# A scale chain issued in two halves around a down column tile, and two pieces of work of the first block pairs written later

## The chip, the cores and the metric

One core of a Trainium2 chip runs the whole program. The metric is device time of one execution in microseconds (us), the median of three runs. Engines are named as in the profile: PE is TensorE (matmul), DVE is VectorE, ACT is ScalarE, POOL is GpSimd, SP is SyncE, which issues most of the DMAs here.

## The reference, cut to what matters

The kernel computes one layer of a streaming encoder on 512 tokens of width 2048: a mixer (a gated recurrence and a band attention), and then a gated feed-forward block with a causal convolution of width 3. Only the second part is touched by the change:

```python
h2 = rms_norm(x, g_ffn[l])
up = causal_dwconv(h2 @ w_up[l], conv_w[l], conv_b[l])      # 2048 -> 2 * 5632
a, gate = jnp.split(up, 2, axis=-1)
x = x + (a * jax.nn.silu(gate)) @ w_down[l]                 # 5632 -> 2048
```

## The kernel before, in words

The feed-forward width 5632 is cut into 44 pairs of 128 channels (128 of `a` and the 128 of `gate` that belong to them). Pairs 0 to 3 are plain: `lead()` multiplies them in f32, and `lead_taps` (L1014) does their convolution taps and gating. Pairs 4 to 43 are block pairs, one `up_unit` each (L988): a product scheme that needs seven `product` calls of 24 matmuls with 256 columns in place of eight. Four pairs make a group, which gives one row block of `w_down`; a group is multiplied in eight down tiles, `down(g, c2)` (L1059), each two column tiles of 12 matmuls with 512 columns. From unit 5 on the order of the steps is fixed as unit, two down tiles, unit, two down tiles and so on (L1086 to L1095); one unit with its two down tiles is called a period here. The last ten down tiles follow unit 43.

All these matmuls run in f16 as a high and a low part. For this every weight tile is split by `split16` (L886): ACT writes the high half (L889), DVE the low half (L890). The scale of a split comes from the largest absolute row sum of the tiles that share it, found by a **scale chain**, `period_scales` (L914): six ACT passes over whole tiles with `accum_out` (`abs_sums`, L895; four tiles of the unit, two raw down tiles, which it loads itself through SP, L876), then in `scales` (L763) a DVE reduction (L770), a diagonal on ACT (L771), one PE product with a matrix of ones (L773) that spreads the sums over the partitions, and small DVE operations (L774 to L776). `m_scale` (L846) does the same for a finished group, and its splits are `m_split` (L853). A tile called `dg` holds the diagonals, in a pool of one buffer; raw down tiles have a pool of three buffers, tag `raw`.

What sets the order: the Python lists `todo`, `ready` and `later`. `todo` holds closures in the order of consumption, nine per period: `start` (the scale chain if the unit has no scale yet, and the split of tile a22), the splits of a11, s1, s2, a12, s4, s3, and the splits of the period's two down tiles. Each closure appends one split tile to `ready`. `take(n)` (L864) runs closures until `ready` has n + 1 entries, and hands out the first:

```python
def take(n_ahead):
    while len(ready) < 1 + n_ahead and todo:
        todo.pop(0)()
    return ready.pop(0)
```

Every `product` (L980) and every `down` (L1060) calls `take(3)`. `start` (L942) reads:

```python
def start():
    if "s" not in u:
        period_scales(j, ds)
    whl("a22")
```

The dict `u` of a unit gets its "s" in `period_scales` alone (L933). `later` is popped once at the end of every product (L985); the taps of pairs 2 and 3 and the scaling of finished groups go through it. The framework schedules each engine's instructions by their place in the program and by when they are ready, and it sets all waits; a tile's buffer goes to the next tile of its tag when its last user is done.

Of the kernel before, what the change touches and what calls it, by code (L numbers as in the profile page):

```python
# [52 lines left out]
def block_kernel(ctx: ExitStack, tc: tile.TileContext, xT, wst, cols, bias_t, masks, yT):  # L53
# [76 lines left out]
    def mm3(ps, sh, sl, mh, ml, start, stop):  # L130
        PE.matmul(ps, lhsT=sh, rhs=mh, start=start, stop=False)  # L131
        PE.matmul(ps, lhsT=sh, rhs=ml, start=False, stop=False)  # L132
        PE.matmul(ps, lhsT=sl, rhs=mh, start=False, stop=stop)  # L133


    colt = cst.tile([P, NC], F32, name="colt")
# [623 lines left out]

    def scales(sets, bound):  # L763


        n = len(sets)
        t = sm_t()
        dg = dgp.tile([P, 2, P], BF16, tag="dg", name=nm("dg"))
        for i, r in enumerate(sets):
            V.tensor_reduce(out=t[:, i:i + 1], in_=r, axis=mybir.AxisListType.X, op=ALU.max)  # L770
            A.activation(dg[:, i], ident, AF.Copy, scale=t[:, i:i + 1])  # L771
        psm = c3(mx_t()[:, 0:2 * P], 2)
        PE.matmul(psm[:, 0:n], lhsT=on1b, rhs=dg[:, 0:n], start=True, stop=True)  # L773
        V.tensor_reduce(out=t[:, 2:2 + n], in_=psm[:, 0:n], axis=mybir.AxisListType.X, op=ALU.max)  # L774
        V.tensor_scalar(out=t[:, 4:4 + n], in0=t[:, 2:2 + n], scalar1=1.01 / bound, scalar2=1e-30, op0=ALU.mult, op1=ALU.add)
        V.reciprocal(out=t[:, 6:6 + n], in_=t[:, 4:4 + n])  # L776
        return [(t[:, 4 + i:5 + i], t[:, 6 + i:7 + i]) for i in range(n)]
# [86 lines left out]
# [4 lines that stand above are left out]
# [25 lines left out]
    def abs_sums(r, tiles):  # L893
        for k, t in enumerate(tiles):
            A.activation(junk_t(), t, AF.Abs, accum_out=r[:, k:k + 1])  # L895
# [13 lines left out]
    def down_loads(ds):  # L909
        at_end = DOWNS.index(ds[0]) - N_BESIDE  # L910
        new = ur_t if at_end >= 0 and at_end % 4 == 0 else raw_t
        return [load(new(), N_DOWN + 8 * g + c2) for g, c2 in ds]

    def period_scales(j, ds):  # L914

        r = sm_t()
        sets = []
        u = units.get(j)
        if u is not None:
            abs_sums(r[:, 0:4], [u[n] for n in ("s1", "a22", "a11", "a12")])  # L920
            sets.append(r[:, 0:4])
        if ds:
            raws = down_loads(ds)
            abs_sums(r[:, 4:8], raws)
            sets.append(r[:, 4:4 + len(ds)])
        sc = scales(sets, BND)
        dt = [(raw, *sc[-1]) for raw in raws] if ds else []
        if u is not None:
            h = cwp.tile([P, 1], F32, tag="uh", name=nm("uh"))
            V.tensor_tensor(out=h, in0=sc[0][0], in1=inv_h, op=ALU.mult)  # L930
            cw = cwp.tile([P, 2, 3], F32, tag="cw", name=nm("cw"))
            A.activation(cw, c3(colt[:, C_CW:C_CW + 3 * 88], 2)[:, :, 3 * j:3 * j + 3], AF.Copy, scale=h)
            u.update(s=sc[0][1], cw=cw, ds=dt)  # L933
        return dt

    def plan_unit(j, ds):
        u = units.setdefault(j, {})

        def whl(n):
            ready.append(split16(u[n], u["s"]))  # L940

        def start():  # L942
            if "s" not in u:
                period_scales(j, ds)
            whl("a22")

        def s2():
            V.tensor_tensor(out=u["a11"], in0=u["s1"], in1=u["a11"], op=ALU.add)  # L948
            whl("a11")

        def s4():
            V.tensor_tensor(out=u["a12"], in0=u["a11"], in1=u["a12"], op=ALU.add)
            whl("a12")
            if j + 1 < NPAIR_FF:
                unit_loads(j + 1)

        def s3():
            i = N_MIX + 16 + 4 * (j - N_LEAD)
            u["s3"] = load_sum(raw_t() if j == N_LEAD else spare, i, i + 2)
            whl("s3")  # L960

        todo.extend([start, lambda: whl("a11"), lambda: whl("s1"), s2, lambda: whl("a12"), s4, s3])
        todo.extend([lambda k=k: down_split(u["ds"][k]) for k in range(len(ds))])

    def down_split(d):
        raw, inv, s = d
        ready.append((split16(raw, s), inv))

    def plan_downs(ds):

        st = []

        def one(k):
            if k == 0:
                st.extend(period_scales(None, ds))
            down_split(st[k])
        todo.extend([lambda k=k: one(k) for k in range(len(ds))])

# [35 lines left out]
    def lead_taps(j, u, out=None):  # L1014
        ys = [taps(u[e], ct, colt[:, C_CW + 3 * ct:C_CW + 3 * ct + 3]) for e, ct in enumerate((j, NPAIR_FF + j))]
        gated(j, *ys, u[0], out=out)
# [7 lines left out]
    def lead():  # L1024
        half = N_LEAD // 2
        n = 0
        for j in range(half):
            u = c3(ur_t(), 2)
            for e in range(2):
                ps = mm_t()  # L1030
                for h in range(2):
                    wh, wl = next_w()
                    for k in range(8):
                        cs = slice(k * P, (k + 1) * P)
                        kt = 8 * h + k
                        mm3(ps, wh[:, cs], wl[:, cs], hh[kt], hl_[kt], kt == 0, kt == KT - 1)
                        if n == 0 and k == 3:
                            finish_r2()
                    if n in (2, 4, 6):
                        t_prep(n // 2 - 1)  # L1040
                    n += 1
                evict_r2(ps, u[:, e])
            lead_taps(j, [u[:, 0], u[:, 1]], (ssa, rmask)[j])
        unit_loads(N_LEAD)
        pss = [mm_t() for _ in range(2 * half)]
        for i in range(8):
            wh, wl = next_w()
            for e, kt in enumerate((i, i + 8)):
                for c in range(2 * half):
                    cs = slice((4 * e + c) * P, (4 * e + c + 1) * P)  # L1050
                    mm3(pss[c], wh[:, cs], wl[:, cs], hh[kt], hl_[kt], i + e == 0, i + e == 8)
            if i in (1, 2, 4, 6, 7):
                t_prep((0, 3, 4, 0, 5, 0, 6, 7)[i])
            if i == 4:
                period_scales(N_LEAD, [])
        us = [evict_r2(ps, actp.tile([P, T], F32, tag="act", name=nm("u"))) for ps in pss]
        later.extend([lambda j=j: lead_taps(half + j, us[2 * j:2 * j + 2]) for j in range(half)])

    def down(g, c2):  # L1059
        t, inv_w = take(3)  # L1060
        mg, parts = groups[g]
        inv = cwp.tile([P, 1], F32, tag="inv", name=nm("inv"))
        V.tensor_tensor(out=inv, in0=inv_w, in1=mg[:, 1:2], op=ALU.mult)
        for cc in range(2):
            c = 2 * c2 + cc
            last = g == NGRP - 1
            ps = mx_t()
            cuts = [slice(0, T)] if not last or c < KT - 1 else [slice(0, H), slice(H, T)]
            pss = [ps] if len(cuts) == 1 else [ps, mx_t()]
            for ps, ts_ in zip(pss, cuts):  # L1070
                for k in range(4):
                    cs = slice((cc * 4 + k) * P, (cc * 4 + k + 1) * P)
                    cl = slice(1024 + (cc * 4 + k) * P, 1024 + (cc * 4 + k + 1) * P)
                    m = parts[k]
                    mm3(ps[:, ts_], t[:, cs], t[:, cl], m[:, ts_], m[:, T + ts_.start:T + ts_.stop], k == 0, k == 3)
            eng = nc.gpsimd if c < KT - 3 else nc.sync
            for ps, ts_ in zip(pss, cuts):
                V.scalar_tensor_tensor(out=acc[c][:, ts_], in0=ps[:, ts_], scalar=inv, in1=acc[c][:, ts_], op0=ALU.mult, op1=ALU.add)  # L1078
                if last:
                    eng.dma_start(out=yT[c][:, ts_], in_=acc[c][:, ts_])  # L1080
# [20 lines left out]
    for st in steps:  # L1101
        if isinstance(st, tuple):
            down(*st)
            continue
        up_unit(st)
        if st == N_LEAD:
            m_scale(0)
            for j in range(4):
                m_split(j)
        elif st % 4 == 3:  # L1110
            g = st // 4
            later.append(lambda g=g: (m_scale(g), m_split(4 * g)))
            later.extend([lambda j=j: m_split(j) for j in range(4 * g + 1, 4 * g + 4)])
        if st == NPAIR_FF - 1:
            while later:
                later.pop(0)()


def _level_masks(np):
# [121 lines left out]
```

## Time and profile before

| | us |
|---|---|
| median of three runs | 2281.39 (2280.96 to 2282.54) |
| the profiled execution, its own time | 2279.07 |
| its span, first to last instruction | 2277.3 |
| stretch 1689.3 to 1808.7 of it | 119.40: four periods |

The own time of the profiled execution is 1.8 us above its span, which is what lies around the program's instructions. Times in the views are counted from the start of the span. The feed-forward part begins near 900 us, the block pairs at 1010.65, and the stretch with steady periods runs from 1089 to 2190.

### The profile page before, as it was taken

To read this page: it belongs to the slowest core of one execution; us is meant where nothing else is said; L and a number is where in the kernel's file an instruction comes from. 1 tells how busy PE (TensorE), PEld (TensorE's weight loads), DVE (VectorE), ACT (ScalarE), POOL (GpSimd) and SP (SyncE) were. 2 spreads that over 40 slices of the span, in tenths; PEclk is the share of its full clock that TensorE was granted. 3 is DMA by queue.
4 is the path that set the end of the run, shared out by engine and by line. 5 is a ranking of instruction groups with operands and counts; after the bars stand their busy time and mean duration, and the time that the engine had idled before them with its cause. 6 is when DMAs were issued, how large, how long until landed. Compare 5 with 4: busy or idle time off the path is not lost.

```text
span 2277.3 us, 34675 instructions
## 1 busy us (share of the span) xinstructions
PE 2200.5 (97%) x13667; PEld 1694.6 (74%) x13667; DVE 1672.4 (73%) x2729; ACT 1336.8 (59%) x2119; POOL 271.3 (12%) x261
## 2 busy tenths in 40 slices
PE   9999999999999999998999999999999999999989
PEld 7888888788888888785667777776776777777654
DVE  7678658857658744787777777787877777778764
ACT  5455445545445424457676767776667776767661
POOL 5223123310001103100000000000000000000001
PEclk9999999999999999999999999999999999999999
DMA  6222222232222333445555565555555666655532
GB/s 211 88 70 75 84 93 65 77 99 84 86 91 93 125 117 101 129 140 131 166 158 164 161 162 162 158 157 153 148 164 158 167 167 167 158 156 160 149 91 83
DMA packets 82755, 294.21 MB, mean 129 GB/s; under 512 B 9568, under 2 KB 10208, under 8 KB 82592
## 3 DMA queue, kind: packets, MB, share of 16 engines
q1 hardware_dynamic: 68112, 240.34, 32.4%
q0 software_dynamic: 14480, 51.65, 12.0%
q8 instruction: 107, 1.75, 0.3%
q14 instruction: 56, 0.46, 0.1%
HBM read 287.76 MB, written 4.19 MB: 128 GB/s over the span
## 4 chain that ended last, share of the span: by engine, by line
PE 49%; DVE 28%; ACT 11%; issue 6%; DMA 6%; POOL 0%; SPq 0%; ACTq 0%; DVEq 0%; POOLq 0%
PE mm L131 12%; PE mm L133 12%; PE mm L132 12%; DVE whl L890 8%; DMA raw<-wst 5%; ACT junk L895 4%; ACT whl L889 4%; DVE vo L1078 3%; PE mx L133 3%; PE mx L131 3%; PE mx L132 3%; DVE vo L828 2%; DVE vo L829 2%; DVE ur L948 1%; ACT dg L771 1%
## 5 line engine op out<-in xcount | busy, mean ns | idle before, releaser
L131 PE MATMUL mm<-th,whl 128*128 128x256 f16 x2240 | 612.5, 273 | 5.9 <-ACT whl L889 5.9
L133 PE MATMUL mm<-th,whl 128*128 128x256 f16 x2240 | 612.3, 273 | 2.6 <-DVE whl L890 2.6
L132 PE MATMUL mm<-tl,whl 128*128 128x256 f16 x2240 | 612.3, 273 | 0.0
L131 PE MATMUL mm<-act,whi 128*128 128x512 f32 x1024 | 406.4, 397 | 0.0
L133 PE MATMUL mm<-act,wlo 128*128 128x512 f32 x1024 | 399.4, 390 | 0.0
L131 PEld LDWEIGHTS <-whl 128*128 128x128 f16 x2948 | 289.1, 98 | 147.9 <-issue 32.0
L132 PE MATMUL mm<-act,whi 128*128 128x512 f32 x1024 | 398.8, 389 | 0.0
L133 PEld LDWEIGHTS <-whl 128*128 128x128 f16 x2948 | 289.2, 98 | 133.7 <-issue 22.5
L132 PEld LDWEIGHTS <-whl 128*128 128x128 f16 x2948 | 289.2, 98 | 108.5 <-issue 0.8
L889 ACT ACTIVATE whl<-ur,sm 128x1024 f16<-128x1024 f32 x206 | 231.1, 1142 | 154.2 <-DVE ur L948 52.1
L119 ACT CAST whi<-raw 128x1024 fp32r<-128x1024 f32 (+1 forms) x161 | 167.7, 1042 | 228.9 <-PE mm L132 183.7
L890 DVE SCALAR_TENSOR_TENSOR whl<-ur,sm,whl 128x1024 f16<-128x1024 f32 x206 | 261.4, 1277 | 41.0 <-ACT whl L889 41.0
L122 DVE TENSOR_TENSOR wlo<-raw,whi 128x1024 fp32r<-128x1024 f32 (+1 forms) x161 | 209.5, 1302 | 91.5 <-ACT whi L119 86.7
L131 PE MATMUL mx<-mhl,whl 128*128 128x512 f16 x708 | 268.5, 379 | 0.0
L132 PE MATMUL mx<-mhl,whl 128*128 128x512 f16 x708 | 268.4, 379 | 0.0
L133 PE MATMUL mx<-mhl,whl 128*128 128x512 f16 x708 | 268.2, 379 | 0.0
L133 PEld LDWEIGHTS mm<-act,wlo 128*128 128x128 f32 x1024 | 192.2, 188 | 41.2
L131 PEld LDWEIGHTS mm<-act,whi 128*128 128x128 f32 x1024 | 192.4, 188 | 38.8 <-issue 0.5
L132 PEld LDWEIGHTS mm<-act,whi 128*128 128x128 f32 x1024 | 192.5, 188 | 38.1 <-issue 0.5
L895 ACT ACTIVATE junk<-ur 128x1024 f16<-128x1024 f32 x146 | 152.1, 1044 | 0.0
L1078 DVE SCALAR_TENSOR_TENSOR vo<-mx,inv,vo 128x512 f32<-128x512 f32 x177 | 130.3, 741 | 25.1 <-PE mx L133 25.1
L890 DVE SCALAR_TENSOR_TENSOR whl<-raw,sm,whl 128x1024 f16<-128x1024 f32 x83 | 106.3, 1283 | 43.1 <-ACT whl L889 42.2
(285 smaller groups left out, 3022.7 us busy)
## 6 DMA issues: line engine op xcount, KB each, us to landing
raw<-wst SPq DMA_DIRECT2D x242, 512.0 KB, 3.5
ur<-wst SPq DMA_DIRECT2D x146, 512.0 KB, 3.5
spare<-wst SPq DMA_DIRECT2D x59, 512.0 KB, 4.8
ur<-wst POOLq DMA_DIRECT2D x40, 512.0 KB, 5.6
spare<-wst POOLq DMA_DIRECT2D x39, 512.0 KB, 8.0
vo<-xT SPq DMA_DIRECT2D x16, 256.0 KB, 5.3
vo<-xT POOLq DMA_DIRECT2D x16, 256.0 KB, 3.1
yT<-vo POOLq DMA_DIRECT2D x13, 256.0 KB, 2.3
```

The lines of the kernel that those rows point to most:

```text
L119: A.copy(out=hi[:, c], in_=raw[:, c])
L122: V.tensor_tensor(out=lo[:, c], in0=raw[:, c], in1=hi[:, c].bitcast(F32), op=ALU.subtract)
L131: PE.matmul(ps, lhsT=sh, rhs=mh, start=start, stop=False)
L132: PE.matmul(ps, lhsT=sh, rhs=ml, start=False, stop=False)
L133: PE.matmul(ps, lhsT=sl, rhs=mh, start=False, stop=stop)
L771: A.activation(dg[:, i], ident, AF.Copy, scale=t[:, i:i + 1])
L828: V.scalar_tensor_tensor(out=y[:, 1:], in0=u[:, :T - 1], scalar=cw[:, 1:2], in1=y[:, 1:], op0=ALU.mult, op1=ALU.add)
L829: V.scalar_tensor_tensor(out=y[:, 2:], in0=u[:, :T - 2], scalar=cw[:, 0:1], in1=y[:, 2:], op0=ALU.mult, op1=ALU.add)
L889: A.activation(t[:, 0:1024], x, AF.Copy, scale=s)
L890: V.scalar_tensor_tensor(out=t[:, 1024:], in0=x, scalar=s, in1=t[:, 0:1024], op0=ALU.mult, op1=ALU.subtract)
L895: A.activation(junk_t(), t, AF.Abs, accum_out=r[:, k:k + 1])
L1078: V.scalar_tensor_tensor(out=acc[c][:, ts_], in0=ps[:, ts_], scalar=inv, in1=acc[c][:, ts_], op0=ALU.mult, op1=ALU.add)
```

## The change

The scale chain is cut into `period_sums` (load the raw down tiles, six sums) and `period_scales` (the rest). For units 6 to 43 a call of `period_sums` is added to the closure of the period's second down tile, and the result is kept in `sums_of`. A call of `period_scales` with it is added in `down`, for the first of a period's two down tiles, behind the matmuls of its first column tile; the product L773 of that call gets an ordering edge behind the last of these matmuls. `start` still computes what it finds missing. The first down tile calls `take(1)` in place of `take(3)`. The taps of pairs 2 and 3 are put further down in `later`, and the scaling of group 0 goes there too; the scaling of group 10 comes after down tiles 77 and 78 in place of directly behind unit 43.

```diff
     def mm3(ps, sh, sl, mh, ml, start, stop):
...
-        PE.matmul(ps, lhsT=sl, rhs=mh, start=False, stop=stop)
+        return PE.matmul(ps, lhsT=sl, rhs=mh, start=False, stop=stop)
...
-    def scales(sets, bound):
+    def scales(sets, bound, after=None):
...
-        PE.matmul(psm[:, 0:n], lhsT=on1b, rhs=dg[:, 0:n], start=True, stop=True)
+        with tc.issue_after(after.ins) if after is not None else ExitStack():
+            PE.matmul(psm[:, 0:n], lhsT=on1b, rhs=dg[:, 0:n], start=True, stop=True)
...
-    def period_scales(j, ds):
+    def period_sums(j, ds):
         r = sm_t()
         u = units.get(j)
         if u is not None:
             abs_sums(r[:, 0:4], [u[n] for n in ("s1", "a22", "a11", "a12")])
...
+        raws = down_loads(ds) if ds else []
+        abs_sums(r[:, 4:8], raws)
+        return j, r, raws
+
+    def period_scales(state, after=None):
+        j, r, raws = state
+        u = units.get(j)
+        sets = ([r[:, 0:4]] if u is not None else []) + ([r[:, 4:4 + len(raws)]] if raws else [])
+        sc = scales(sets, BND, after)
+        dt = [(raw, *sc[-1]) for raw in raws]
...
         def start():
             if "s" not in u:
-                period_scales(j, ds)
+                period_scales(period_sums(j, ds))
             whl("a22")
...
-        todo.extend([lambda k=k: down_split(u["ds"][k]) for k in range(len(ds))])
+        for k in range(len(ds)):
+            todo.append(lambda k=k: down_split(u["ds"][k]))
+        if ds and j + 1 < NPAIR_FF:
+            def sums(f=todo.pop()):
+                f()
+                sums_of[j + 1] = period_sums(j + 1, DOWNS[2 * (j - N_LEAD):2 * (j - N_LEAD) + 2])
+            todo.append(sums)
+
+    sums_of = {}
...
-        later.extend([lambda j=j: lead_taps(half + j, us[2 * j:2 * j + 2]) for j in range(half)])
+        later.extend([lambda: None] * 3)
+        later.append(lambda: lead_taps(half, us[0:2]))
+        later.extend([lambda: None] * 3)
+        later.append(lambda: lead_taps(half + 1, us[2:4]))
+        later.append(lambda: (m_scale(0), m_split(0), m_split(1)))
+        later.append(lambda: (m_split(2), m_split(3)))
 
     def down(g, c2):
-        t, inv_w = take(3)
+        i = DOWNS.index((g, c2))
+        first = i % 2 == 0 and i < N_BESIDE - 2
+        t, inv_w = take(1 if first else 3)
...
-                    mm3(ps[:, ts_], t[:, cs], t[:, cl], m[:, ts_], m[:, T + ts_.start:T + ts_.stop], k == 0, k == 3)
+                    last_mm = mm3(ps[:, ts_], t[:, cs], t[:, cl], m[:, ts_], m[:, T + ts_.start:T + ts_.stop], k == 0, k == 3)
+            if first and cc == 0:
+                j = N_LEAD + 2 + i // 2
+                period_scales(sums_of.pop(j), last_mm)
...
             down(*st)
+            if st in DOWNS[N_BESIDE - 1:N_BESIDE + 1] and later:
+                later.pop(0)()
+                while later and st == DOWNS[N_BESIDE]:
+                    later.pop(0)()
             continue
         up_unit(st)
-        if st == N_LEAD:
-            m_scale(0)
-            for j in range(4):
-                m_split(j)
-        elif st % 4 == 3:
+        if st % 4 == 3:
...
-        if st == NPAIR_FF - 1:
-            while later:
-                later.pop(0)()
```

`N_LEAD` is 4, `NPAIR_FF` 44 and `N_BESIDE` 78; `product` is not in the diff.

## Rows read from the trace of the kernel before

**Rows 1.** The page, section 1: the span, and each engine's busy time, share and instructions.

```profile
span 2277.3 us, 34675 instructions
...
PE 2200.5 (97%) x13667; PEld 1694.6 (74%) x13667; DVE 1672.4 (73%) x2729; ACT 1336.8 (59%) x2119; POOL 271.3 (12%) x261
```

**Rows 2.** What PE waited for (us, times, longest) in 1005:1089, then 1089:2190, then 2190:2278.

```profile
PE mm L131 <- ACT whl L889: 5.9, 3, 3.3
PE mm L133 <- DVE whl L890: 2.6, 2, 1.6
PE mx L773 <- ACT dg L771: 2.1, 3, 1.5
...
PE mx L773 <- ACT dg L771: 35.0, 30, 2.0
...
PE mx L773 <- ACT dg L771: 9.7, 1, 9.7
```

**Rows 3.** Busy us (instructions) of PE, PEld, DVE, ACT, POOL; granted clock; DMA share; GB/s.

```profile
1689.30:1808.70 119.40, 116.68 (x878) 85.67 (x877) 94.29 (x143) 83.75 (x126) 6.99 (x8) 1.00 0.58 161
...
1010.00:1089.00 79.00, 68.41 (x528) 53.06 (x527) 59.07 (x92) 56.42 (x90) 4.70 (x6) 0.94 0.59 161
...
2203.30:2213.40 10.10, 4.63 (x12) 1.73 (x12) 6.85 (x15) 5.60 (x11) 0.00 (x0) 0.50 0.12 44
```

**Rows 4.** PE in order of time in one period: first product, end of the sixth, L773.

```profile
1702.72 0.27 PE L131 MATMUL mm<-th,whl 128*128 128x256 f16 x1
...
1718.33 0.27 PE L133 MATMUL mm<-th,whl 128*128 128x256 f16 x1
1718.85 0.27 PE L773 MATMUL mx<-dg,on1b 128*128 128x256 bf16 x1 [0.25 <-ACT dg L771]
```

**Rows 5.** The chain of waits from one L773 to the next: start us, us, what.

```profile
1689.73 0.18 PE mx L773
...
1690.91 1.14 ACT whl L889
...
1693.95 1.19 DVE whl L890
...
1699.41 0.66 DVE vo L1078
...
1702.52 1.13 DVE ur L948
...
1710.37 1.29 DVE whl L890
...
1711.68 5.33 DMA raw<-wst
...
1717.03 1.15 ACT junk L895 x2
1718.18 0.63 ACT dg L771 x2
...
1718.85 0.28 PE mx L773
```

**Rows 6.** DVE in order of time, same period: split of the second raw down tile.

```profile
1713.48 1.28 DVE L890 SCALAR_TENSOR_TENSOR whl<-raw,sm,whl 128x1024 f16<-128x1024 f32 x1 [1.83 <-ACT whl L889]
```

**Rows 7.** ACT's groups in the four periods 1689.3:1808.7 (busy us, mean ns).

```profile
L895 ACT ACTIVATE junk<-ur 128x1024 f16<-128x1024 f32 x14 | 14.6, 1043 | 0.0
...
L771 ACT ACTIVATE dg<-ident,sm 128x128 bf16<-128x128 f32 x10 | 3.7, 394 | 0.0
```

**Rows 8.** Loads to landing: raw tiles in those four periods; unit tiles, whole span (median).

```profile
DMA to landing us min/median/max: 5.0/5.7/8.3
...
ur<-wst SPq DMA_DIRECT2D x146, 512.0 KB, 3.5
```

**Rows 9.** PE in order of time behind the last unit: the product of group 10's scale.

```profile
2208.77 0.27 PE L773 MATMUL mx<-dg,on1b 128*128 128x128 bf16 x1 [9.67 <-ACT dg L771]
```

More of the change, by code (lines that the diff above doesn't have):

```diff
@@ L912, in down_loads @@
         return [load(new(), N_DOWN + 8 * g + c2) for g, c2 in ds]
-    def period_scales(j, ds):
+    def period_sums(j, ds):
         r = sm_t()
-        sets = []
         u = units.get(j)
@@ L920, in period_scales @@
             abs_sums(r[:, 0:4], [u[n] for n in ("s1", "a22", "a11", "a12")])
[L921 to L927, printed above, removed]
+        raws = down_loads(ds) if ds else []
[7 more added lines that the diff above has]
+        dt = [(raw, *sc[-1]) for raw in raws]
         if u is not None:
@@ L974, in one @@
             if k == 0:
-                st.extend(period_scales(None, ds))
+                st.extend(period_scales(period_sums(None, ds)))
             down_split(st[k])
@@ L1054, in lead @@
             if i == 4:
-                period_scales(N_LEAD, [])
+                period_scales(period_sums(N_LEAD, []))
         us = [evict_r2(ps, actp.tile([P, T], F32, tag="act", name=nm("u"))) for ps in pss]
-        later.extend([lambda j=j: lead_taps(half + j, us[2 * j:2 * j + 2]) for j in range(half)])
+        later.extend([lambda: None] * 3)
[4 more added lines that the diff above has]
+        later.append(lambda: (m_split(2), m_split(3)))
     def down(g, c2):
-        t, inv_w = take(3)
+        i = DOWNS.index((g, c2))
+        first = i % 2 == 0 and i < N_BESIDE - 2
+        t, inv_w = take(1 if first else 3)
         mg, parts = groups[g]
```

## The prediction

> **What bounds the kernel now.** I read the page first: ACT is busy for 59% of the span [rows 1], which says little, since the stages differ. The table of stretches is the better view. In four steady periods, 119.40 us or 29.85 us each, PE issues almost without a break at the full granted clock, DVE is busy for 94.29 us and ACT for 83.75 us [rows 3]. One period's matmuls alone need 168 x 0.109 (15.61 us for 143 steps [rows 4]) + 48 x 0.218 (twice the columns) = 28.8 us, so about 1.1 us per period is PE standing still. The view of waits names it: from 1089 to 2190 PE waits 35.0 us in 30 waits, all for L771, the diagonal in front of L773 [rows 2]. The time order shows where: the first product of a unit begins at 1702.72, 144 matmuls or six products later comes the last one at 1718.33, and then L773, with its wait, ahead of the seventh product [rows 4].
>
> Why the diagonal is late is told by the chain of waits. From one L773 (1689.73) to the next (1718.85) it never leaves one loop: the scale, the splits of the unit's weights one after another on DVE, the split of the first down tile at 1710.37, a load of 5.33 us that needed its buffer, the sum over the loaded tile, the diagonals, L773 [rows 5]. So the period is the length of this loop, a little more than PE's own work, and ACT's and DVE's shares don't show it.
>
> Two more losses stand outside. Behind unit 43 PE waits 9.67 us for the scale of the last group [rows 9], and in 10.1 us around that the granted clock is 0.50, 1.2 GHz [rows 3]. In the first units PE waits 5.9 + 2.6 + 2.1 = 10.6 us [rows 2] and has a mean clock of 0.94 over 79 us [rows 3].
>
> **What the change does to the steady periods.** It is meant to take L773 out of the seventh product's way. Walk the lists. After each `take(3)` three tiles are ready. The seventh product of a unit therefore runs the closure with index 9 of the period, counted from 0, and that is `start` of the next unit. The closure with index 8, run by the sixth product, has just made `sums_of` for that unit, but "s" is set by `period_scales` alone, and the added call of it is in the down tile, which comes later. So `start` finds no "s" and does the whole chain as before: loads, sums, diagonals, L773. The old chain stays, and 38 times (units 6 to 43) a second one is added. L773 with 256 columns should be there 77 times instead of 39.
>
> Per period this adds:
> - **ACT:** six sums of 1.04 us, two diagonals of 0.39 us and one small scaling [rows 7], some 7.3 us beside 83.75 / 4 = 20.9 us, thus 28.2 us. It fits in 29.85 only if ACT hardly waits.
> - **DVE:** two reductions, the handling of the spread sums and a column, some 0.9 us beside 23.6 us.
> - **PE:** one product, 0.11 us. The added one stands behind the first down column tile and its sums were started a closure earlier, so no PE wait of its own is counted; its cover is the 7.8 us of column tiles behind it.
> - **SP and DMA:** two loads of 512 KB, 1.05 MB beside about 4.8 MB. At a DMA share of 0.58 [rows 3] there is room. Behind them on SP wait the next unit's loads. POOL's accumulating loads are not moved past anything.
> - **The raw buffers:** this is the dear part. There are three. The tiles loaded by `period_sums` in closure 8 are those that the splits use in the end, as the later `period_scales` overwrites the list, so they hold two buffers until their splits. The two loads of `start` then share the third one. The first of them gets a buffer when the second down tile of the period has been split, the second only when the first has been summed. Before, one load was in the loop [rows 5]; now there are two, one after the other. ACT waits in order for the second; behind that sum stand the diagonals and whatever the schedule has put there, the unit's taps perhaps, for which DVE waits.
>
> The new loop, from rows. From L773 to the end of the second down tile's split: 1.18 us to the first split (1689.73 to 1690.91), 1.14 on ACT, then on DVE nine splits of 1.19, two sums of 1.13, two evictions of 0.66 [rows 5], and 0.90 for the second chain's handover (the same 1.18 without the product): 1.18 + 1.14 + 10.71 + 2.26 + 1.32 + 0.90 = 17.5 us. Now this stretch takes 1714.76 - 1689.73 = 25.0 us (1713.48 + 1.28 [rows 6]); I take the lower figure because what else DVE does in it, the unit's combining, taps and evictions, needs nothing of the chain and can run ahead of the later L773. From that split to the next L773: load 5.33, sum 1.15, load 5.33, sum 1.15, diagonals 0.63, 0.1 of gaps: 13.7 us. Sum 31.2 us, 1.35 us over 29.85, and 38 x 1.35 = **+51 us**. PE's 35.0 us of waits don't go away; they grow into about 2.5 us per period, split between L773 and the first product of the next unit.
>
> Bounds. The load: 5.0 to 8.3 us for raw tiles, median 5.7, and 3.5 for the unit's tiles [rows 8]. Two at 3.5 give 27.5 us, less than PE and ACT need; then the period is some 29.3, a loss of nothing and a gain of 0.5 us. Two at 8.3 give 37.1 us, +277 us. The stretch before it: 17.5 to 25.0 + 1.2, so that all together may be 39.9 us per period, +382 us. I take 5.33, since that row is the same load in the same place.
>
> A rule of the Trainium skill bears on this load. "DMA: Bandwidth & Descriptors", section "Anatomy of one DMA", puts a DMA at about 2.0 us plus bytes by 436 GB/s, an estimate of 3.2 us here. By it the two loads would cost 6.4 us, not 10.7, the loop would fall under PE's own work, and the steady part would gain rather than lose; the measured loads, none under 5.0 us, disagree, and I go by them.
>
> **The two other parts.** The scale of group 10 is now written behind down tile 77. Its chain takes 9.67 us behind the seventh product, and two down tiles cover 48 x 0.218 = 10.5 us; so PE's wait goes, and with it the 4.6 us of matmuls at half clock, 2.3 us: **-12.0 us**. If the cover fell short by the matmul that it is behind, 1 to 2 us of wait would stay; late next would be the splits of group 10, which have another 10.5 us. In the first units the taps of pairs 2 and 3 leave the first two products and group 0's scale leaves unit 4, but all of it comes back in units 4 and 5, where DVE is what PE waits for [rows 2]. At best 10.6 + 0.06 x 79 = 15.3 us are saved, at worst some 8 us of moved DVE work delays unit 5; I take **-3 us**.
>
> The `take(1)` and the edge cost nothing by themselves: they move two splits behind the second chain, which the 17.5 us hold. Sum: 2279.07 + 51 - 12 - 3 = 2315 on the profiled execution, which is 2.3 us under the median of the runs: **2317 us**.
>
> **Rivals.**
> - *The doubled chain hides; faster.* ACT waits 36 us in four periods, 9 us each, and 7.3 us fit in. It decides whether the stretch of 13.7 us comes to under 12.3, by faster loads or because the first of the two gets its buffer a period ahead. Then only the ends count: 2281 - 15 = 2266, or down to 2247 with 0.5 us of gain per period. For it: loads of 3.5 us exist. Against: three buffers, four tiles. Chance 0.15. The rule of the DMA page above would end here.
> - *The chain moves as the words say* (the change does what it says). If `start` found its scale, 35.0 us of waits would go as well: 2281 - 50 = 2231. Against it is the count of the closures. Chance 0.03.
> - *The DVE work does not move ahead.* The schedule is static, so the combining and the taps may stay behind L773; the loop is then up to 39.9 us, 2281 - 15 + 382 = 2648. Against: they are ready when the seventh product ends, some 7 us ahead of the new L773. Chance 0.07.
> - *The clock falls each period.* After the wait of 9.67 us PE had the lower level of 1.2 GHz for 10.1 us [rows 3, 9]; a wait of 2.0 us, 30 times, left the full clock. If the new, longer waits do the same, a period pays up to the 2.3 us of the end: 2317 + 38 x 2.3 = 2404. Chance 0.10. "TensorE: Matmul & The Clock Gate" of the Trainium skill, section "HAM oscillation", describes a kernel that pays this in every tile; whether waits of 2.5 us do so, no run here shows.
>
> **How the numbers follow.** My forecast, the loop of 31.2 us, has 0.65, with its own range 2275 to 2375. A measurement here tells about 0.2%, 4.6 us, from no change. Faster holds the first two rivals but for their upper edge: 0.17. Within 0.2%: 0.05, the edge between the first rival and the forecast. Slower: 0.78. The range goes from 2262, which takes in most of the first rival, to 2430, which takes in the clock rival and a loop of 34.2 us; the second and third rival stay outside.
>
> **What would show it.** Right: L773 with 256 columns 77 times, 76 more loads of raw tiles, 228 more sums; steady periods of 31 us or more, and a chain of waits with two raw loads between two L773; ACT near 28 us per period; no wait of 9.67 us behind unit 43. Wrong: L773 only behind down column tiles, or PE without waits for L771 at periods under 29 us.

## The result, and the profile after

The changed kernel takes **2633.79 us** (median of four runs, 2629.89 to 2637.47) beside 2281.18 for the kernel before on the same chip: a ratio of 1.155 (95% interval 1.153 to 1.157), 353 us slower. The forecast was 2317, the range 2262 to 2430. The direction was right, the size was wrong by a factor of ten (353 against 36 us), and the range did not hold it. In the changed kernel the lines have moved by one and later by more: L774 is the old L773, L890 and L891 are the two halves of a split, L896 is a sum, L1100 an eviction; in kernels of the experiments they move by up to two more.

The page, section 1, of the profiled execution (2637.47 us), against [rows 1]; then the view of one tile (the diagonals' product on PE), from the page and the view of all groups the sums, and from the page the DMA issues of raw tiles:

```profile
span 2635.7 us, 35767 instructions
...
PE 2282.0 (87%) x13705; PEld 1716.4 (65%) x13705; DVE 1718.7 (65%) x2957; ACT 1608.6 (61%) x2689; POOL 272.6 (10%) x261
```

```profile
L774 PE MATMUL mx<-dg,on1b x95: 216/273/418, 922.2 to 2606.2; 128*128 128x256 bf16 x77, 128*128 128x128 bf16 x18
```

```profile
L896 ACT ACTIVATE junk<-ur 128x1024 f16<-128x1024 f32 x279 | 290.4, 1043 | 0.0
...
L896 ACT ACTIVATE junk<-raw 128x1024 f16<-128x1024 f32 x158 | 165.8, 1050 | 101.0 <-DMA raw<-wst 100.0
...
L896 ACT ACTIVATE junk<-spare 128x1024 f16<-128x1024 f32 x39 | 40.7, 1043 | 0.0
...
raw<-wst SPq DMA_DIRECT2D x318, 512.0 KB, 3.5
```

The counts are the ones foretold: 77 products with 256 columns, 318 raw loads (242 before), 279 + 158 + 39 = 476 sums (248 before, so 228 more). The old chain has stayed and a second one has come.

What PE waited for in 1005:1089, 1089:2545 and 2545:2636, against [rows 2]:

```profile
PE mm L131 <- ACT whl L890: 13.3, 1, 13.3
PE mx L774 <- ACT dg L771: 9.9, 2, 8.5
PE mm L133 <- DVE whl L891: 3.4, 3, 2.1
...
PE mx L774 <- ACT dg L771: 296.9, 37, 10.0
...
PE mx L774 <- ACT dg L771: 8.1, 2, 5.7
```

In the steady part nearly every period has one wait of about 8 us for the diagonal (37 waits, 296.9 us), where the kernel before had 30 short ones of 35.0 us together. Stretches of the changed kernel, columns as in [rows 3]: the steady part, one period in two pieces (from L774 to the end of the second down tile's split, and from there to the next L774), and the first 5.4 us behind L774:

```profile
1089.00:2190.00 1101.00, 876.64 (x6146) 615.10 (x6145) 697.49 (x1168) 785.72 (x1296) 48.94 (x56) 0.89 0.52 148
...
1899.47:1924.24 24.77, 24.70 (x154) 15.71 (x154) 18.57 (x27) 15.91 (x25) 0.26 (x1) 0.88 0.43 142
1924.24:1939.57 15.33, 7.22 (x68) 6.33 (x66) 5.42 (x14) 11.51 (x22) 0.61 (x1) 0.88 0.43 114
...
1899.50:1904.90 5.40, 5.36 (x14) 1.94 (x14) 2.91 (x7) 3.17 (x7) 0.00 (x0) 0.50 0.34 97
```

The period is 40.1 us here (24.77 + 15.33), ACT works 27.4 us in it, no engine is full, and behind the wait PE has the lower level of its clock, 1.2 GHz. The chain of waits over the same period, with start, duration and what, shows why:

```profile
1899.54 0.37 PE mx L774
1899.91 0.43 PE mx L131
...
1905.03 0.21 PE mx L774
1905.25 0.31 PE mx L131
...
1913.11 0.11 PE mm L131
...
1918.39 0.37 ACT su L1009
1918.76 1.05 ACT whl L890
1919.81 1.22 ACT junk L896 x3
...
1922.96 1.29 DVE whl L891
1924.27 8.51 DMA raw<-wst
...
1932.87 1.15 ACT junk L896 x2
1934.04 3.62 DMA raw<-wst
...
1937.74 1.16 ACT junk L896 x2
```

Read it as one loop. The first chain's L774 stands on PE in front of the whole down pair: 12 matmuls of the first column tile at half clock (0.43 us each), the second L774, 36 more, 13.6 us in all, before the next unit's first product (1913.11) can start. Two products later the splits of the down tiles come, the second ends at 1924.24, this frees a raw buffer, and only then the first raw load of the next chain starts. Two loads and two sums, one after the other, follow, and the next L774 at 1939.57. PE, with its products done at 1931.5, has waited 8.1 us. From the first product of unit 6 to that of unit 43, 37 periods, the changed kernel takes 1450.0 us, 39.2 each, and the kernel before 1106.5, 29.9 each. These 343.5 us are nearly all of the 358.4 by which the two profiled spans differ; 17.0 us lie ahead of unit 6, and behind unit 43's first product the changed kernel is 2.1 us faster. PE in order of time, the two places that are used below (the wait stands in the brackets):

```profile
1899.54 0.37 PE L774 MATMUL mx<-dg,on1b 128*128 128x256 bf16 x1 [7.70 <-ACT dg L771]
...
1912.95 0.27 PE L131 MATMUL mm<-th,whl 128*128 128x256 f16 x1
```

### The profile page after: what moved, and what is told of

The parts are those of the page before. It is cut to its first block, busy times and chain, and to the rows that moved or that the text cites. A ratio compares the mean times of both kernels' runs of the same rounds, so it can differ in the third digit from the quotient of the medians.

```text
span 2635.7 us, 35767 instructions
## 1 busy us (share of the span) xinstructions
PE 2282.0 (87%) x13705; PEld 1716.4 (65%) x13705; DVE 1718.7 (65%) x2957; ACT 1608.6 (61%) x2689; POOL 272.6 (10%) x261
## 4 chain that ended last, share of the span: by engine, by line
PE 53%; ACT 16%; DMA 15%; DVE 13%; issue 4%; POOL 0%; SPq 0%; ACTq 0%; DVEq 0%; POOLq 0%
DMA raw<-wst 13%; PE mm L131 10%; PE mm L133 10%; PE mm L132 10%; ACT junk L896 9%; PE mx L131 6%; PE mx L132 6%; PE mx L133 6%; DVE whl L891 5%; ACT whl L890 3%; ACT mhl L857 1%; DMA ur<-wst 1%; DVE wlo L122 1%; PE mx L774 1%; DVE vo L1100 1%
## 5 line engine op out<-in xcount | busy, mean ns | idle before, releaser
L131 PE MATMUL mm<-th,whl 128*128 128x256 f16 x2240 | 611.5, 273 | 13.3 <-ACT whl L890 13.3
L131 PEld LDWEIGHTS <-whl 128*128 128x128 f16 x2948 | 294.6, 100 | 460.8 <-issue 353.1
L133 PEld LDWEIGHTS <-whl 128*128 128x128 f16 x2948 | 294.9, 100 | 135.8 <-issue 36.7
L132 PEld LDWEIGHTS <-whl 128*128 128x128 f16 x2948 | 296.0, 100 | 122.2 <-issue 28.4
L890 ACT ACTIVATE whl<-ur,sm 128x1024 f16<-128x1024 f32 x206 | 232.6, 1141 | 230.9 <-DVE sm L777 112.2
L891 DVE SCALAR_TENSOR_TENSOR whl<-ur,sm,whl 128x1024 f16<-128x1024 f32 x206 | 260.7, 1278 | 77.9 <-ACT whl L890 77.9
L774 PE MATMUL mx<-dg,on1b 128*128 128x256 bf16 (+1 forms) x95 | 29.8, 314 | 314.9 <-ACT dg L771 314.9
L131 PE MATMUL mx<-mhl,whl 128*128 128x512 f16 x708 | 301.3, 426 | 0.0
L132 PE MATMUL mx<-mhl,whl 128*128 128x512 f16 x708 | 297.5, 420 | 0.0
L133 PE MATMUL mx<-mhl,whl 128*128 128x512 f16 x708 | 295.7, 418 | 0.0
L896 ACT ACTIVATE junk<-ur 128x1024 f16<-128x1024 f32 x279 | 290.4, 1043 | 0.0
L896 ACT ACTIVATE junk<-raw 128x1024 f16<-128x1024 f32 x158 | 165.8, 1050 | 101.0 <-DMA raw<-wst 100.0
```

The lines of the kernel that those rows point to most:

```text
L133: return PE.matmul(ps, lhsT=sl, rhs=mh, start=False, stop=stop)
L890: A.activation(t[:, 0:1024], x, AF.Copy, scale=s)
L891: V.scalar_tensor_tensor(out=t[:, 1024:], in0=x, scalar=s, in1=t[:, 0:1024], op0=ALU.mult, op1=ALU.subtract)
```

## The experiments

Fourteen runs, in the order of the questions. Ratios are to the kernel before on the same chip; its medians beside these runs lie within 2.1 us of each other, so times are compared across chips too.

**1. Are the two ends worth 15 us?** The kernel before, with only the two moved pieces of the head and the tail.

```diff
-        later.extend([lambda j=j: lead_taps(half + j, us[2 * j:2 * j + 2]) for j in range(half)])
+        later.extend([lambda: None] * 3)
+        later.append(lambda: lead_taps(half, us[0:2]))
...
+            if st in DOWNS[N_BESIDE - 1:N_BESIDE + 1] and later:
+                later.pop(0)()
```

> The kernel before with the two moved pieces of work alone: taps of pairs 2 and 3, scale of group 0, scale of group 10. Forecast of the prediction: 9.67 us of wait and 2.3 us of half clock go at the end, 3 us at the head, so 2266 us. Rival (the same work comes back in units 4 and 5): head loses 8 us, time about 2277. Steady periods stay at 29.85 us either way.

2282.42 us, ratio 1.0005 (0.9992 to 1.0019): nothing, and above the numbers of forecast and rival. Its PE waits in 1005:1089 and behind unit 43, first of three rows and the only row:

```profile
PE mm L131 <- ACT whl L889: 13.3, 1, 13.3
...
PE mx L773 <- ACT dg L771: 8.1, 2, 5.7
```

The wait of 9.67 us [rows 9] is gone from group 10's product and 8.1 us stand at two other scale products near the end. In the head the waits of 10.6 us have become 13.3 + 2.8 + 1.4 = 17.5 us. The traces part the two ends. From unit 43's first product to the end of the span pass 96.8 us before and 96.9 here: the tail gains nothing. Unit 6's first product comes at 1074.1 before and at 1079.9 here: the head loses 5.8 us. So all but a few us of the changed kernel's loss come from the chains.

**2. One chain in place of two.** The seventh product of units 5 to 42 keeps two tiles ready in place of three, so that `start` comes after the added call and finds its scale.

```diff
-        product(bank[2][:, H:], T3)
+        product(bank[2][:, H:], T3, 2 if N_LEAD < j < NPAIR_FF - 1 else 3)
```

> The changed kernel, with the seventh product of units 5 to 42 asking for two tiles ahead in place of three, so that the next unit's start runs behind the added call and finds its scale. Theory (the doubled chain is the whole loss): L774 with 256 columns 39 times, none of PE's waits for L771 left in the steady part, periods of 28.8 to 29.1 us against 29.85, the ends worth 12 to 15 us: 2225 to 2250 us. Rival (the chain placed behind a column tile is late whoever calls it, and delays the next unit's splits): periods stay at 30 us or more and the time at 2281 or above.

2359.92 us, ratio 1.0345 (1.0319 to 1.037). The doubling costs 274 of the 353 us. But the single chain, behind the first column tile as the change's words say, is still slower than before; the rival was right. Its waits of PE in 1089:2190, and then its chain of waits:

```profile
PE mx L774 <- ACT dg L771: 43.8, 33, 4.1
PE mm L133 <- DVE whl L891: 27.6, 49, 0.9
PE mm L131 <- ACT whl L890: 10.0, 7, 3.8
```

```profile
1824.07 6.08 DMA raw<-wst
...
1831.44 0.70 DVE z L1017
...
1834.49 0.34 DVE sm L775
1834.82 0.66 DVE vo L830
1835.48 0.66 DVE vo L829
1836.14 0.08 DVE sm L776
1836.22 0.65 DVE vo L1100
...
1838.44 1.05 ACT whl L890
```

The product runs at 1832.1, the first split that needs its scale at 1838.4: 6.3 us, where the kernel before took 1.2 [rows 5]. The three small DVE operations L775 to L777 stand between the unit's taps (L829, L830) and an eviction (L1100), in DVE's order, and the splits behind them free the raw buffer later.

**3. The same chain ahead of the column tile.** The added call is put in front of the first down tile's matmuls, without the edge.

```diff
+        if first:
+            period_scales(sums_of.pop(N_LEAD + 2 + i // 2))
         mg, parts = groups[g]
...
-            if first and cc == 0:
-                j = N_LEAD + 2 + i // 2
-                period_scales(sums_of.pop(j), last_mm)
```

> The kernel of e1, but the added call stands ahead of the first column tile, without the ordering edge, so that L774 comes between the seventh product and the down tile, 2.6 us earlier than in e1 and 2.6 us later than in the kernel before. Theory (each us by which L774 comes later is paid, by the handover that falls among the taps): between before and e1, 2290 to 2335. Rival (only the place behind the column tile hurts): 2266 to 2285.

2255.59 us, ratio 0.989 (0.9869 to 0.9911): 104 us under experiment 2, faster than the kernel before, and faster than theory and rival had it. DVE in order of time behind the product, which runs at 1826.4, and ACT's first split:

```profile
1827.19 0.41 DVE L775 TENSOR_REDUCE sm<-mx 128x2 f32<-128x256 f32 x1
...
1828.64 0.17 DVE L777 RECIPROCAL sm<-sm 128x2 f32<-128x2 f32 x1
```

```profile
1829.85 3.21 ACT L890 ACTIVATE whl<-ur,sm 128x1024 f16<-128x1024 f32 x3
```

The handover takes 3.5 us and is ahead of the taps. Steady periods are 28.8 us, PE's own work, and one in four, which holds a group's scale product, 30.1. In 1089:2170 PE waits 8.3 us for the diagonal, at clock 1.00.

**4. Buffers.** A fourth buffer for raw tiles (the activations give up two of 48), in four kernels.

```diff
+    rawp = ctx.enter_context(tc.tile_pool(name="rawp", bufs=4))
...
-        raw = wp.tile([P, 1024], F32, tag="raw", name=nm("raw"))
+        raw = rawp.tile([P, 1024], F32, tag="raw", name=nm("raw"))
```

In the changed kernel:

> The changed kernel, both chains, with four raw buffers. Theory (the second of the extra loads stands in the loop since it needs the buffer of the first, 3.6 + 1.2 us per period): 2634 falls to 2440 to 2530, as in the run with one load. Rival (loads hide, sums and PE's place set the loop): 2600 to 2635.

2504.3 us: 130 us gained, as expected.

In the kernel before:

> The kernel before with four buffers for the raw tiles in place of three (paid with two of the 48 buffers of the tag act). Theory (the period of before is a loop that holds one raw load of 5.3 us, since the second raw tile of a period needs the buffer of the first one just split): the load leaves the loop, PE's 35 us of waits for L771 in the steady part fall under 10, time 2240 to 2260. Rival (the loop only moves to the sums over the unit's own tiles, or to DVE): waits of 20 us or more stay, 2270 to 2282.

2259.78, ratio 0.9923 (0.9893 to 0.9954), within the theory's times. Its profiled execution (2272.59, 13 us above its other three) still has 18.2 us of PE waits for the diagonal in 1089:2190, where under 10 were expected.

With one chain behind the column tile:

> The kernel of e1 (one chain per period, product behind the column tile) with four raw buffers. Theory (e1 is slow because L774 comes some 5 us later and the loop of before, with its raw load, closes behind it): without the load the loop is about 25 us and hidden, PE waits little, 2230 to 2260. Rival (e1 is slow because the scale's handover on DVE and ACT now stands among the taps and comes 6.2 us behind L774 in place of 1.2, and the next unit's splits are late for PE): waits for whl stay near the 37 us of e1, time 2300 to 2340.

2275.97, 84 us under experiment 2 and between theory and rival.

With one chain ahead of it:

> The version with the added call ahead of the first column tile, and four buffers for raw tiles in place of three. Theory: with the product between the seventh product and the down tile, what is left of PE's waits in the steady part (8.3 us in 18 waits for the diagonal) is the raw load that waits for its buffer; the fourth buffer takes it away: 2244 to 2250 us, and no steady wait for the diagonal over 0.5 us in all. Rival: nothing of the loop is left there and the buffer only moves transfers: 2253 to 2258 us, as without it.

2255.42, nothing; the rival was right, though the 8.3 us of small waits stay. So the raw load is in the loop in the first three kernels, and out of it in the fourth, where PE's own work is the limit. It also carries most of what the place costs: moving the chain from behind the column tile to ahead of it saves 104 us with three buffers and 21 with four (2275.97 to 2255.42).

**5. What of the doubled chain costs?** Four edits of the changed kernel. First the raw tiles loaded once:

```diff
-                period_scales(period_sums(j, ds))
+                period_scales(period_sums(j, ds, sums_of[j][2] if j in sums_of else None))
```

> The changed kernel, but start takes the raw down tiles that the added call has already loaded; it sums them again, so twelve sums per period stay, and the two extra loads of 512 KB go. Theory (of the 15.3 us from the second down split to L774, the second load behind the first sum takes 3.6 + 1.2 us and the first one waits for a buffer): that stretch falls to about 10 us, then set by ten sums of 1.04 on ACT, the period to 34 us, the time to 2420 to 2450. Rival (the six extra sums on ACT are the loss): no change, 2620 to 2640.

2527.62 us, 106 us gained, less than expected. Then the scale product with a PSUM buffer of its own, so that the down tiles' matmuls can be put in front of it:

```diff
-        psm = c3(mx_t()[:, 0:2 * P], 2)
+        psm = c3(ps_sc.tile([P, T], F32, tag="sc", name=nm("sc"))[:, 0:2 * P], 2)
```

> The changed kernel, with the scale product's PSUM tile under a tag of its own (one buffer, the down tiles keep three), so that nothing but readiness orders L774 against the down tiles. Both chains stay. Theory (L774 stands in front of the down tiles because their PSUM tiles come after its own in the same pool, and that puts 10.4 us of down tiles plus half clock into the loop behind it): down matmuls run ahead of L774, the stretch from L774 to the end of the second down split falls from 24.4 us to 17.5 to 19, the period from 39.5 to 33 us, the time to 2370 to 2400. Rival (place on PE does not matter, the two loads and twelve sums set the period): period 39 us, time 2620 to 2640.

2540.74 us, 93 us gained, between the two. In the compiled order 33 to 48 of a pair's down matmuls now stand ahead of the product; with the shared tag none did. Both at once:

> The changed kernel with both cures: start takes the raw tiles that the added call loaded, and the scale product has a PSUM buffer of its own. What is left of the doubled chain are the sums, the diagonals, the product and the small DVE work, twice. Theory: loads and place lie one behind the other in one loop, so what each saved alone (106 and 93 us) adds up: 2420 to 2450 us. Rival: the loop falls under PE's own work before both are used up, and the kernel ends near the one with a single chain behind the column tile: 2340 to 2390 us.

2468.67 us: 165 us gained, less than theory (184 to 214) and rival had it. Its chain of waits shows what is left:

```profile
1755.41 8.14 DMA raw<-wst
1763.57 7.38 ACT junk L898 x14
...
1772.29 0.37 PE sc L776
```

Seven sums run on ACT one after another between the load and the diagonal: the second set of sums is in the loop too. So the sums were made once as well, with the second diagonal, product and handover kept, without and with the buffer of its own:

```diff
-                period_scales(period_sums(j, ds))
+                period_scales(sums_of[j] if j in sums_of else period_sums(j, ds))
```

> The changed kernel; start takes the row sums and the raw tiles of the added call, so loads and sums are made once; diagonals, product and small DVE operations stay doubled, and both products keep their places. Theory: the six sums stand in the loop (7.4 us of ACT between a raw load and the diagonal in the chain of waits of the run with loads and place cured), so against the run with loads alone made once (2528 us) some 38 x 3 to 5 us go: 2340 to 2415 us. Rival: ACT does the second sums beside other work and the place in front of the down tiles decides: 2500 to 2530 us.

2416.03 us, ratio 1.059 (1.048 to 1.069), 218 us gained, a microsecond above the theory's range.

> The same, and the scale product in a PSUM buffer of its own. Theory: loads, sums and place are all there is to the doubled chain; what is left is a second diagonal, product and handover, cheap: 2290 to 2370 us, at or under the kernel with a single chain behind the column tile (2360). Rival: the second product behind the first column tile costs as much as the sums do, whatever feeds it: 2420 to 2470 us.

2457.11 us: with the buffer of its own it is 41 us worse, as the rival's number has it. Where these 41 us come from was not followed. In both runs the scheduler puts the first product back between the sixth and the seventh in most periods. In the run without the buffer its handover is short (1774.1 to the first split at 1775.2); the second one's is not. DVE of this run, whose second product is at 1779.4:

```profile
1780.59 0.42 DVE L775 TENSOR_REDUCE sm<-mx 128x2 f32<-128x256 f32 x1
...
1783.62 0.16 DVE L777 RECIPROCAL sm<-sm 128x2 f32<-128x2 f32 x1
...
1785.88 1.28 DVE L891 SCALAR_TENSOR_TENSOR whl<-ur,sm,whl 128x1024 f16<-128x1024 f32 x1
```

4.2 us pass from the second product to L777, the taps and evictions between. The run without the buffer has 56 us more than experiment 2. More work it has only in the second diagonal, product and handover; these, and the other place of the first product, were not parted further. The place of the product has no price of its own: its buffer saves 93 us where the chain is very late, 59 with the loads made once, and costs 41 with loads and sums made once.

**6. The sums earlier, the product at its old place.** One chain; `start` takes the sums of the closure before it, the call in `down` is left out, and every `down` calls `take(3)` again.

```diff
-                period_scales(period_sums(j, ds))
+                period_scales(sums_of.pop(j) if j in sums_of else period_sums(j, ds))
```

> One chain per period, at the old place: start takes the sums that the closure before it has made, no call in the down tile, take(3) everywhere. Theory: the chain still begins when the second down tile's split frees the raw buffer, so writing the sums one closure earlier gives little, and the product still stands in front of the seventh product: 2270 to 2284 us. Rival: the earlier sums by themselves take the diagonal's wait away: 2245 to 2258 us, as with the product moved ahead of the down tile.

2283.31 us, ratio 1.0014 (1.0005 to 1.0023): the sums in two halves bring nothing without the other place.

**7. The best version.** Experiment 3 with the fourth buffer, and the head as before the change.

> The same, and the taps of pairs 2 and 3 and the scaling of group 0 back at their old places. Theory: the late writing of these pieces costs what the waits in the first units grew by, from 10.6 to about 17.7 us; undone, the time is 5 to 8 us under the version without this edit. Rival: what the head gains comes back as DVE and ACT work in the first units (as the two ends together were worth nothing): within 3 us of it.

**2247.39 us, ratio 0.985** (0.983 to 0.987), 8 us under the same without this edit: the late writing of the head's pieces costs what PE's waits there grew by. Its first row of PE's waits in 1000:1089 (13.4 us without this edit), and its steady part:

```profile
PE mm L132 <- ACT whl L891: 7.2, 4, 4.3
```

```profile
1089.00:2160.00 1071.00, 1062.61 (x7979) 779.94 (x7978) 858.93 (x1306) 745.96 (x1146) 62.42 (x72) 1.00 0.58 162
```

The tail's part was not run alone; here 97.3 us pass from unit 43's first product to the end of the span, so it shows no gain beside the 96.8 before.

**The account.** From 2634 us: loads and sums made once, with the place that the product then takes, 218; the second product and handover, 56; the product ahead of the column tile, 104. This comes to 2256, 25 under the kernel before. The shares hold for this order of steps: the experiments with the buffers show that they depend on each other.

## Why the prediction was wrong

- **The doubled chain** was right, from the count of the closures alone: 38 added chains, 76 loads, two raw loads in the chain of waits, ACT near 28 us per period. The rival that the change does what its words say was right to be held small, but its price was wrong: such a kernel takes 2360 us, not 2231 (experiment 2). I had priced the new place by the wait that it removes and not by the handover that it puts among DVE's taps.
- **The step that failed** is the 17.5 us from L773 to the end of the second down tile's split. I chose the lower end as "what else DVE does in it ... can run ahead of the later L773". The combining and the taps did run ahead, the evictions of the down tiles stayed. DVE of the changed kernel in the period above, whose L774 is at 1939.57:

```profile
1931.58 0.68 DVE L1017 TENSOR_TENSOR z<-mm,su 128x512 f32<-128x512 f32 x1
...
1936.42 0.74 DVE L830 SCALAR_TENSOR_TENSOR vo<-z,cw,vo 128x510 f32<-128x510 f32 x1
```

  And yet the stretch measured 24.8 us, as long as before, where the forecast had 17.5. These 7.3 us are most of the 8.9 by which this period (40.1) is longer than the 31.2 foretold. It is not a sum of DVE work: PE sets it. Split tiles lie in six buffers (two tags of three), and a split waits until a product has read what lay there before. In the chain of waits above, ACT's copy L1009 waits for the second product of the unit, and the two down splits follow it. A split of the same unit that waits for a matmul, in ACT's order of time:

```profile
1915.82 1.15 ACT L890 ACTIVATE whl<-spare,sm 128x1024 f16<-128x1024 f32 x1 [1.73 <-PE mm L133]
```

  The second down split ends 11.3 us after the unit's first product in the changed kernel (1924.24 - 1912.95) and 12.0 before (1714.76 - 1702.72, [rows 4, 6]). It is so in all 38 periods from unit 6 to 43: 11.3 or 12.3 us in the changed kernel, whose periods go from 37.5 to 41.3, and 11.5 to 13.2 before. (With a late handover it doesn't hold: in experiment 2 it is 13.7 to 21.7.) So the stretch is the way from L774 to the next unit's first product plus these 11 to 12 us. Before, that way was the seventh product and the down pair, 13.0 us [rows 4, 5]; now it is the down pair with its half clock, 13.4 (1912.95 - 1899.54). The rows to see this were all there: the same split against the first product of its unit, in several periods, would have said that it follows PE.
- **The loads** were nearly right in sum: 8.51 + 3.62 measured where 5.33 + 5.33 was taken, and 15.3 us for the whole piece against 13.7. By the Trainium skill, "DMA: Bandwidth & Descriptors", section "Anatomy of one DMA", the prediction had an estimate of 3.2 us; the second load is near it, the first is not. The section states its fit for DMAs that GpSimd issues, and these loads are issued by SP, which the prediction left out.
- **The added product without a PE wait of its own** was right, the wait of "about 2.5 us per period" was 8.
- **"The clock falls each period"** was held a rival at 0.10 and happened as well: the first column tile runs at clock 0.50 behind the wait, and the steady part has a mean of 0.89. It costs 12 x (0.43 - 0.22) = 2.5 us per period, some 96 us in 38, near the 2.3 us of that rival; as the tile stands behind L774 in the chain of waits, it lies in the loop. This is an estimate: no run kept the two chains and the full clock. The row behind this rival was misread: the 30 waits of the kernel before were 2.0 us at most and 1.2 in the mean [rows 2]. The Trainium skill, "TensorE: Matmul & The Clock Gate", section on HAM oscillation, describes a kernel that is re-throttled in every tile behind its wait for data; the trace agrees, with a wait of 7.70 us and 0.50 behind it.
- **"The DVE work does not move ahead"**, 2648 us, came within 14 us of the result by luck, and was wrong as a mechanism: the combining and the taps did move ahead. It ends there since it took the other end of the same bound.
- **The ends**: -12 us in the tail were nothing (96.8 us before, 96.9 in experiment 1), as the wait moved on to two later scale products (8.1 us, where 9.7 had been); -3 us in the head were +5.8.
- **The range** took 0.65 for a loop of 31.2 us with an upper end of 34.2, though the bounds in the text reached 39.9. The lower end rested on one argument without a row; it should not have narrowed the range.

## What to carry to other kernels

Before a stretch of the chain of waits is worked out as a sum of one engine's work, look at what its end follows from period to period; if that is another engine's progress, taking work out of the stretch doesn't shorten it. When a small product is moved past large ones, its followers on the other engines move as well: look where the handover then stands in their order. And a second call that makes what the first still makes is found by walking the lists; what it costs is found by asking which buffers both hold.

## What was not expected of the hardware

A product of 0.27 us, moved with its followers by 2.6 us of PE work, made 104 us of difference in 38 periods. The lower clock behind the wait (1.2 GHz for 5.4 us behind 7.70 us) is a second price on top of the wait, and it falls on the matmuls that the loop goes through. The first of the two raw loads took 8.51 us and the second, of the same size in the same period, 3.62. Why the first one is so slow is not shown: it runs beside other loads, but no run took these away.
